# Three arms by row count in a mixture-of-experts loop, each stage in two branches, weight splits seven halves ahead

## Chip, cores, metric

One core of one Trainium2 chip. The metric is the device time of one execution in microseconds; lower is better. The time before is the median of three runs.

## What is computed

A block with a gated-MLP and a linear-attention half, then a routed mixture of 64 experts with D = 1024 and an inner width of 512, over 2048 tokens, two experts for each token, everything in float32. The part that matters:

```python
def hier_moe(t, wrg, brg, wre, bre, w1, w3, w2):
    ...
    gate = p_top * jax.nn.softmax(l_top, axis=-1)
    expert = g_idx * EXPERTS_PER_GROUP + e_local
    ...
    def expert_block(args):
        xblk, e = args
        hblk = jax.nn.silu(xblk @ w1[e]) * (xblk @ w3[e])
        return hblk @ w2[e]
    ...
    yb = yb * buf_gate[:, None].astype(yb.dtype)
    return jax.ops.segment_sum(yb, buf_tok, num_segments=T + 1)[:T]
...
h = h + g2 * y.reshape(Bn, S, D)
return rmsnorm(h, g_final)
```

## The kernel before

Up to about 1040 us the kernel computes the two mixing halves and the routing: for each expert a list of its token rows (`idx`), its gates, and the number of blocks of 128 rows (`nblk`). The loop over 64 experts follows, and from about 2363 us the final norm. The change lies in the loop.

**An expert's matrices.** `w_e` holds 12 k-tiles of 128 x 1024 for each expert: eight for up (w1 and w3 side by side, 512 columns each) and four for down. SP loads each k-tile into one of 28 raw tiles in rotation (`wload`, L611). Half a tile, 512 columns, is one *half*: 16 halves in up, 8 in down.

**Splits.** Float32 products are made of three matmuls in a rounded format, fp32r. ScalarE rounds a raw half to `wh` (L80), VectorE subtracts to get the rest `wl` (L81); both lie in a ring of eight pairs. The rows are split likewise: `xhe` and `xle` for up, `hhe` and `hle` for down. `mm3` (L84 to L86) then issues xh wh, xh wl and xl wh into one PSUM bank. `need(p)` issues all splits up to half p; `block` calls it four halves ahead of the matmuls.

**Order.** One pass is up(e+1), weight loads, the count of the next expert, a gather of rows by POOL (`gath`, L1162), down(e). `xprep` (L1195 to L1199) transposes the gathered rows of expert e+2 on TensorE and splits them; it stands in the middle of down(e), ahead of its fifth half. `htr` (L1203) transposes the gated result of expert e+1 ahead of the seventh half, and `hsplit` (L1207, L1208) splits it in the middle of the next up. `glu` (L1211, L1212) is silu on ScalarE and a product on VectorE; `yevac` (L1217) scales down's result by the gate; `scat` (L1220) adds its rows into DRAM, an indirect DMA issued by POOL. Each engine runs its instructions in this order.

**Arms.** `up` and `down` have two versions behind a branch on `nblk[e]` that every engine takes: `one` for at most 128 rows, `two` for a second block, whose matmuls follow three halves behind and use the same splits. `PA`, `PY`, `TP` and `TH` are pairs of PSUM banks.

Of the kernel before, what the change touches and what calls it, by code (L numbers as in the profile page):

```python
# [8 lines left out]
F32 = mybir.dt.float32  # L9
# [8 lines left out]
P = 128  # L18
# [12 lines left out]
def kernel(ctx: ExitStack, tc: tile.TileContext, a: dict, out: bass.AP):  # L31
# [1147 lines left out]
    vec.tensor_scalar(nblk, ci_, 7, None, op0=OP.logical_shift_right)  # L1179
    most = wk.tile([1, 1], I32, name="most")  # L1180
# [45 lines left out]
    LA = R - LAG - 1  # L1226
# [5 lines left out]
    def need(p):  # L1232
        nonlocal nsp
        while nsp <= min(p, len(hseq) - 1):
            e, k, i = hseq[nsp]
            split_w(W[e, k][:, i * 512:(i + 1) * 512], *ring[nsp % R])
            nsp += 1

    def both(two, one):

        nonlocal nsp
        n0 = nsp
        two()
        n1, nsp = nsp, n0
        yield
        one()
        assert nsp == n1
# [8 lines left out]
    def block(base, n, outs, hls, at):  # L1256

        for q in range(n + (LAG if len(outs) > 1 else 0)):
            if q < n:
                need(base + q + LA)  # L1260
                if q in at:
                    at[q]()
# [27 lines left out]
    def rest():  # L1290
# [22 lines left out]
    def up(e):  # L1313

        at = {4: lambda: hsplit(TH[0], hx)} if e else {}
        base = hpos[e, 0, 0]

        def two():
            xprep(xq[e % 2], rows2(e), PY)
            block(base, 2 * KD, (PA, TP), (xhl, rows2(e)), at)  # L1320
            glu(PA, sh)
            glu(TP, sh2[e % 2])

        def one():
            block(base, 2 * KD, (PA,), (xhl,), at)
            glu(PA, sh)

        g = both(two, one)
        with tc.If(NB_[e] > 1, preferred_fallthrough_block=False) as f:
            next(g)  # L1330
        with f.Else():
            next(g, None)

    def down(e):

        base = hpos[e, KD, 0]
        at = {}
        if e + 2 < NE:
            at[4] = lambda: xprep(xg[(e + 2) % 3], xhl, TP)
# [3 lines left out]
        def two():
            htr(sh2[e % 2], TH[1])
            hsplit(TH[1], hx2)
            block(base, 2 * KF, (PY, PA), (hx, hx2), at)
            yevac(PA, col(gate, NE + e), y2)
            scat(y2, col(idx, NE + e))

        def one():  # L1350
            block(base, 2 * KF, (PY,), (hx,), at)

        g = both(two, one)
        with tc.If(NB_[e] > 1, preferred_fallthrough_block=False) as f:
            next(g)
        with f.Else():
            next(g, None)
# [6 lines left out]
    need(LA - 1)  # L1364
# [48 lines left out]
def _layout(inp):  # L1413
# [29 lines left out]
    z["w_e"] = np.concatenate([w13, w2], axis=1).transpose(0, 2, 1, 3).reshape(NE, P, 12 * D)  # L1443
# [30 lines left out]
```

## Time and profile before

| what | us |
|---|---|
| median of 3 runs | 2416.13 (2415.8 to 2416.62) |
| the profiled execution | 2418.95 |
| its span | 2417.3 |
| PE busy | 2279.6 (94%) |
| DVE busy | 1929.6 (80%) |
| ACT busy | 1438.4 (60%) |
| POOL busy | 727.9 (30%) |
| mean granted TensorE clock | 0.969 |

Engines are PE (TensorE), DVE (VectorE), ACT (ScalarE), POOL (GpSimd) and SP (which issues DMAs). A pipelined instruction shows longer than the distance to the next one's start; that distance is what it costs its engine. A row's bracket holds the idle time just before it and what ended it. [...] Busy shares over the span mix the phases; the loop is read from its own windows.

### The profile page before, as it was taken

How to read it: one execution, taken by the hardware profiler on the slowest of the kernel's cores; microseconds unless marked ns; L12 is line 12 of the kernel's file. 1: busy time of each engine (PE TensorE's matmuls, PEld its weight loads, DVE VectorE, ACT ScalarE, POOL GpSimd, SP SyncE). 2: the span in 40 equal slices, each digit the busy share in tenths (PEclk: the TensorE clock that was granted, in tenths of full speed). 3: DMA queues.
4: the chain of work that ended last, by engine and by line, in shares of the span. 5: the costliest groups of instructions: out<-in, count | busy, mean ns of one | idle time of the engine just before them, and what ended most of it. 6: DMA issues, size and time to landing. Idle time of an engine off the chain costs nothing.

```text
span 2417.3 us, 40083 instructions
## 1 busy us (share of the span) xinstructions
PE 2279.6 (94%) x11932; PEld 1879.8 (78%) x11932; DVE 1929.6 (80%) x4302; ACT 1438.4 (60%) x2731; POOL 727.9 (30%) x602
## 2 busy tenths in 40 slices
PE   8999999999999899889999999999999999999980
PEld 3888888978777788778777888888777788888870
DVE  4555566567786788789887899999686699999986
ACT  3544443433323222378776788888575588888873
POOL 1123311147673122237521122323131232322220
PEclk9899999999999999989999999999999999999995
DMA  7333332256664654589998899999996799999947
GB/s 273 110 102 100 106 108 97 97 179 213 221 221 155 233 209 177 184 309 377 332 305 263 285 379 371 367 353 347 328 322 192 219 360 371 369 357 357 364 144 295
DMA packets 193220, 613.42 MB, mean 254 GB/s; under 512 B 36557, under 2 KB 36685, under 8 KB 192854
## 3 DMA queue, kind: packets, MB, share of 16 engines
q1 hardware_dynamic: 152358, 516.56, 58.8%
q0 software_dynamic: 38048, 87.95, 12.3%
q10 hardware_dynamic: 2448, 4.46, 0.5%
q8 instruction: 178, 2.92, 0.5%
q14 instruction: 188, 1.54, 0.2%
HBM read 547.42 MB, written 102.28 MB: 269 GB/s over the span
## 4 chain that ended last, share of the span: by engine, by line
PE 33%; DVE 12%; DMA 7%; issue 5%; ACT 0%; DVEq 0%; another core or an unknown queue 0%; SPq 0%; POOLq 0%; ACTq 0%; POOL 0%
DVE wl L81 9%; PE pa L84 6%; PE pa L86 6%; PE pa L85 6%; DMA we<-in_w_e_dram 4%; PE py L86 3%; PE py L84 3%; PE py L85 3%; DMA accD<-y,idx 2%; PE tpe L1195 1%; DVE y L1217 1%; PE tpe L85 1%; PE tpe L84 1%; PE tpe L86 1%; DMA hf<-accD 1%
## 5 line engine op out<-in xcount | busy, mean ns | idle before, releaser
L81 DVE TENSOR_TENSOR wl<-we,wh 128x512 fp32r<-128x512 f32 x1536 | 954.2, 682 | 83.6 <-ACT wh L80 77.0
L80 ACT ACTIVATE wh<-we 128x512 fp32r<-128x512 f32 x1536 | 892.4, 630 | 146.9 <-DVE wl L81 46.4
L84 PE MATMUL pa<-wh,xhe 128*128 128x512 f32 x1024 | 403.4, 394 | 9.5 <-ACT wh L80 6.3
L86 PE MATMUL pa<-wh,xle 128*128 128x512 f32 x1024 | 399.9, 391 | 0.0
L85 PE MATMUL pa<-wl,xhe 128*128 128x512 f32 x1024 | 399.5, 390 | 0.0
L1220 POOL DMA_INDIRECT accD<-y,idx x71 | 238.8, 3364 | 530.7 <-DVE y L1217 446.7
L84 PEld LDWEIGHTS pa<-wh,xhe 128*128 128x128 f32 x1024 | 192.3, 188 | 69.9 <-issue 28.5
L86 PEld LDWEIGHTS pa<-wh,xle 128*128 128x128 f32 x1024 | 192.3, 188 | 40.7
L85 PEld LDWEIGHTS pa<-wl,xhe 128*128 128x128 f32 x1024 | 192.5, 188 | 37.6
L84 PE MATMUL py<-wh,hhe 128*128 128x512 f32 x512 | 213.7, 417 | 6.9 <-ACT wh L80 6.4
L1162 POOL DMA_INDIRECT xg<-hnD,idx x64 | 93.5, 1461 | 417.2 <-DVE wl L81 143.2
L86 PE MATMUL py<-wh,hle 128*128 128x512 f32 x512 | 202.9, 396 | 1.6 <-issue 1.3
L85 PE MATMUL py<-wl,hhe 128*128 128x512 f32 x512 | 201.3, 393 | 3.2 <-DVE wl L81 3.2
L86 PEld LDWEIGHTS py<-wh,hle 128*128 128x128 f32 x512 | 97.3, 190 | 25.7 <-issue 3.4
L349 POOL TENSOR_SCALAR sc<-sc,dec 64x128 f32<-64x128 f32 x140 | 111.4, 795 | 19.1 <-PE po L682 7.8
L84 PEld LDWEIGHTS py<-wh,hhe 128*128 128x128 f32 x512 | 97.5, 190 | 24.8 <-issue 6.3
L85 PEld LDWEIGHTS py<-wl,hhe 128*128 128x128 f32 x512 | 97.8, 191 | 16.0 <-issue 0.2
L1070 POOL DMA_INDIRECT tabD<-pair,ri x32 | 70.0, 2187 | 91.3 <-DMA tabD<-pair,ri 58.8
L86 PE MATMUL pmx<-hi,mld 128*128 128x512 f32 x224 | 89.6, 400 | 5.6 <-DVE mld L81 5.6
L1217 DVE SCALAR_TENSOR_TENSOR y<-py,gate,g2b 128x512 f32<-128x512 f32 x128 | 89.7, 740 | 4.1 <-PE py L86 4.1
L84 PE MATMUL pmx<-hi,mhd 128*128 128x512 f32 x224 | 91.4, 408 | 0.4 <-ACT mhd L80 0.4
L85 PE MATMUL pmx<-lo,mhd 128*128 128x512 f32 x224 | 88.6, 396 | 0.0
(417 smaller groups left out, 4660.1 us busy)
## 6 DMA issues: line engine op xcount, KB each, us to landing
we<-in_w_e_dram SPq DMA_DIRECT2D x765, 512.0 KB
wt<-in_w_modB_dram SPq DMA_DIRECT2D x32, 512.0 KB
kve<-kveD SPq DMA_DIRECT2D x48, 256.0 KB
wt<-in_w_modA_dram SPq DMA_DIRECT2D x16, 512.0 KB
x<-in_x_dram SPq DMA_DIRECT2D x16, 512.0 KB
xD<-xf POOLq DMA_DIRECT2D x32, 256.0 KB
mfd<-mxD SPq DMA_DIRECT2D x16, 512.0 KB
xd<-in_x_dram SPq DMA_DIRECT2D x16, 512.0 KB
```

Of the source, the lines that this page charges most:

```text
L80: act.activation(hi, raw, AF.Copy)
L81: vec.tensor_tensor(lo, raw, hi.bitcast(F32), op=OP.subtract)
L84: pe.matmul(o, lh, wh, start=start, stop=False)
L85: pe.matmul(o, lh, wl, start=False, stop=False)
L86: pe.matmul(o, ll, wh, start=False, stop=stop)
L349: pool.tensor_scalar(s1[64:128, hs], s0[64:128, hs], dec[64:128, ci, h:h + 1], None, op0=OP.mult)
L1070: pool.indirect_dma_start(out=tabD, out_offset=bass.IndirectOffsetOnAxis(ap=ri[:, i:i + 1], axis=0), in_=pair[:, i], in_offset=None)
L1162: pool.indirect_dma_start(out=x, out_offset=None, in_=hnD, in_offset=bass.IndirectOffsetOnAxis(ap=ix, axis=0), bounds_check=S - 1, oob_is_ ...
L1195: pe.transpose(four(tp[c // 4])[:, c % 4], x[:, c * P:(c + 1) * P], ident)
L1217: vec.scalar_tensor_tensor(y[:, c], py[i], gt, g2b[:, c], op0=OP.mult, op1=OP.mult)
L1220: pool.indirect_dma_start(out=accD, out_offset=bass.IndirectOffsetOnAxis(ap=ix, axis=0), in_=y, in_offset=None, bounds_check=S - 1, oob_is ...
```

## The change

A third arm, `few`, serves experts with at most 64 rows. `xx` holds the low part of the first 64 rows beside the high part of all 128, so that one matmul with `wh` or `wl` (`block2`) makes both products: two matmuls a half instead of three. The result's two halves of partitions are added in `glu2`. The low part comes into `xx` by a POOL copy at the end of `xprep`, for every expert. In down, the last halves are neither split nor rounded: plain float32 matmuls out of the raw tiles with `hf`, a float32 copy of the transposed gated rows; four of eight halves in few, two in one, none in two. Each stage is cut in two branches of half the length. Splits go up to seven halves ahead (four in two); one or two halves of up are held back until after the silu (`held`). `w_e` is laid out with each k-tile in one piece, and 27 raw tiles rotate instead of 28. `nhalf` counts blocks of 64 rows. In the changed kernel the lines are: branches L1263 and L1264, `few`'s matmuls L1306, `glu2`'s three VectorE operations L1312, L1314 and L1316, `xprep`'s L1206, its POOL copy L1208, `hsplit` L1219, `glu` L1224, `yevac` L1229, `scat` L1232, the counts L1320 and L1328.

```diff
-    NW, NR = 25, 28
+    NW, NR = 25, 27
...
-            eng.dma_start(out=W[e, k], in_=a["w_e"][e, :, k * D:(k + 1) * D])
+            eng.dma_start(out=W[e, k], in_=a["w_e"][e, k])
...
-    xhl = [wk.tile([P, KD, P], F32R, name=n) for n in ("xhe", "xle")]
+    LO, HI = slice(0, P // 2), slice(P // 2, P)
+    xx = wk.tile([P, KD, P // 2 + P], F32R, name="xhe")
+    xhl = [xx[:, :, P // 2:], wk.tile([P, KD, P], F32R, name="xle")]
...
+        if hl is xhl:
+            pool.tensor_copy(xx[:, :, LO], xl[:, :, LO].bitcast(F32))
...
         act.activation(hh, four(th), AF.Copy)
+        if th is TH[0]:
+            act.activation(hf, four(th)[:, 2:4], AF.Copy)
...
-    LA = R - LAG - 1
...
-    def both(two, one):
+    def arms(e, two, one, few):
...
+        with tc.If(NB_[e] > 1, preferred_fallthrough_block=False) as f:
+            with tc.If(NB_[e] > 2, preferred_fallthrough_block=False) as g:
+                arm(two)
+            with g.Else():
+                arm(one)
+        with f.Else():
+            arm(few)
...
+    def block(base, n, span, top, outs, hls, at=(), raw=0):
...
+            need(base + min(q + R - 1 - lag, top), raws)
...
+                if p < n - raw:
+                    mms(o[p % 2], hl, p // 2, p % 2, n // 2, ring[(base + p) % R])
+                else:
+                    e, k, i = hseq[base + p]
+                    pe.matmul(o[i], hf[:, p // 2 - 2], W[e, k][:, i * 512:(i + 1) * 512], start=False,
+                              stop=p // 2 == n // 2 - 1)
...
+    def block2(base, n, span, top, at):
+
+        for q in range(*span):
+            need(base + min(q + R - 1, top))
+            if q in at:
+                at[q]()
+            for j, w in enumerate(ring[(base + q) % R]):
+                pe.matmul(PA[q % 2], xx[:, q // 2, 0:P], w, start=q < 2 and j == 0, stop=q // 2 == n // 2 - 1 and j == 1)
+
+    def glu2(t, between):
+
+        act.activation(t[HI], PA[0][HI], AF.Copy)
+        act.activation(sh[HI], PA[1][HI], AF.Copy)
+        vec.tensor_tensor(sh[LO], PA[0][LO], t[HI], op=OP.add)
+        act.activation(sh[LO], sh[LO], AF.Silu)
+        vec.tensor_tensor(t[LO], PA[1][LO], sh[HI], op=OP.add)
+        between()
+        vec.tensor_tensor(sh[LO], sh[LO], t[LO], op=OP.mult)
...
     def up(e):
...
+        ends = {KD: KD + R - 2, n: n + 3}
+        for span in ((0, KD), (KD, n)):
+            top = ends[span[1]]
+            held = lambda: need(base + n + 3)
...
+            def few():
+                block2(base, n, span, top - (span[1] == n), at)
+                if span[1] == n:
+                    glu2(sh2[e % 2], held)
+
+            arms(e, two, one, few)
...
     def down(e):
...
+        for span in ((0, KF), (KF, n)):
+            top = span[1] + R - 2
...
+            arms(e, two, lambda: block(base, n, span, top, (PY,), (hx,), raw=2),
+                 lambda: block(base, n, span, top, (PY,), (hx,), raw=4))
+            if span[0] == 0 and e + 2 < NE:
+                xprep(xg[(e + 2) % 3], xhl, TP)
         if e + 1 < NE:
-            at[6] = lambda: htr(sh, TH[0])
...
+            htr(sh, TH[0])
...
-    need(LA - 1)
+    need(R - 2)
```

Three places show the order of the instructions. First VectorE at the end of up, before (`wl` are splits, `she` is the gated product):

```order
L81 TENSOR_TENSOR wl_11208<-we_9492,wh_11207 128x512
L81 TENSOR_TENSOR wl_11210<-we_9492,wh_11209 128x512
L81 TENSOR_TENSOR wl_11212<-we_9494,wh_11211 128x512
L81 TENSOR_TENSOR wl_11214<-we_9494,wh_11213 128x512
L1212 TENSOR_TENSOR she<-she,pa_11183 128x512
L1329 UNCONDITIONAL_BRANCH
```

and now, in the few arm of the second branch of up:

```order
L1263 COMPARE_AND_BRANCH
L81 TENSOR_TENSOR wl_11225<-we_11146,wh_11224 128x512
L81 TENSOR_TENSOR wl_11211<-we_11175,wh_11210 128x512
L81 TENSOR_TENSOR wl_11213<-we_11175,wh_11212 128x512
L81 TENSOR_TENSOR wl_11215<-we_11177,wh_11214 128x512
L1312 TENSOR_TENSOR she<-pa_11180,sh_11206 64x512
L1314 TENSOR_TENSOR sh_11206<-pa_11181,she 64x512
L81 TENSOR_TENSOR wl_11217<-we_11177,wh_11216 128x512
L1316 TENSOR_TENSOR she<-she,sh_11206 64x512
L1263 UNCONDITIONAL_BRANCH
```

Two additions of half height have come in ahead of the product, and one split, the held one, stands between them and it.

Second VectorE in down around `xprep` (`xle`), before:

```order
L81 TENSOR_TENSOR wl_11222<-we_11179,wh_11221 128x512
L81 TENSOR_TENSOR wl_11208<-we_8756,wh_11207 128x512
L1199 TENSOR_TENSOR xle<-tpe_11184,xhe 128x512
L1199 TENSOR_TENSOR xle<-tpe_11185,xhe 128x512
L81 TENSOR_TENSOR wl_11210<-we_8756,wh_11209 128x512
L81 TENSOR_TENSOR wl_11212<-we_8758,wh_11211 128x512
L81 TENSOR_TENSOR wl_11214<-we_8758,wh_11213 128x512
L1354 UNCONDITIONAL_BRANCH
```

and now, with the few arm's second branch of down behind it:

```order
L1206 TENSOR_TENSOR xle<-tpe_11182,xhe 128x512
L1206 TENSOR_TENSOR xle<-tpe_11183,xhe 128x512
L1263 COMPARE_AND_BRANCH
L81 TENSOR_TENSOR wl_11217<-we_8948,wh_11216 128x512
L81 TENSOR_TENSOR wl_11219<-we_9128,wh_11218 128x512
L81 TENSOR_TENSOR wl_11221<-we_9128,wh_11220 128x512
L81 TENSOR_TENSOR wl_11223<-we_9130,wh_11222 128x512
L1263 UNCONDITIONAL_BRANCH
```

`xprep` has moved out of the branch to the seam between its two; four splits follow the last `xle` instead of three, and the two `y` come next in both kernels.

Third POOL in down, before (`xq` and the first `accD` are for a second block, in branches of their own):

```order
L1162 DMA xq_10938<-hnD,idx 128x1024
L1272 UNCONDITIONAL_BRANCH
L1354 COMPARE_AND_BRANCH
L1354 ISA
L1354 UNCONDITIONAL_BRANCH
L1220 DMA accD<-y_10939,idx 2048x1024
L1354 UNCONDITIONAL_BRANCH
L1220 DMA accD<-y_11206,idx 2048x1024
```

and now:

```order
L1162 DMA xq_11164<-hnD,idx 128x1024
L1322 UNCONDITIONAL_BRANCH
L1263 COMPARE_AND_BRANCH
L1263 UNCONDITIONAL_BRANCH
L1264 COMPARE_AND_BRANCH
L1264 UNCONDITIONAL_BRANCH x2
L1208 CAST xhe<-xle 128x8x64
L1263 COMPARE_AND_BRANCH
L1263 ISA
L1263 UNCONDITIONAL_BRANCH
```

The copy stands behind the gather and between the two branches of down, ahead of the scatter.

## Rows read from the trace of the kernel before

**Rows 1.** This is the table of windows of the expert loop and of the end: window, its length, busy us (x instructions) of PE, PEld, DVE, ACT and POOL, then PEclk (granted clock of TensorE), DMA share, GB/s.

```profile
1400.00:1500.00 100.00, 98.90 (x462) 80.45 (x461) 100.00 (x166) 88.21 (x158) 30.45 (x11) 1.00 1.01 376
2375.00:2412.00 37.00, 0.00 (x0) 0.00 (x0) 33.53 (x111) 16.11 (x29) 0.00 (x0) 0.50 0.98 396
```

**Rows 2.** This is the timeline of VectorE over one expert with at most 128 rows: start us, us from the first start to the last end, engine, line, operation, out<-in, count.

```profile
1405.11 3.09 DVE L81 TENSOR_TENSOR wl<-we,wh 128x512 fp32r<-128x512 f32 x5
1408.12 0.68 DVE L1208 TENSOR_TENSOR hle<-th,hhe 128x512 fp32r<-128x512 f32 x1
1408.72 6.70 DVE L81 TENSOR_TENSOR wl<-we,wh 128x512 fp32r<-128x512 f32 x11
1415.35 0.68 DVE L1212 TENSOR_TENSOR she<-she,pa 128x512 f32<-128x512 f32 x1
1415.94 3.09 DVE L81 TENSOR_TENSOR wl<-we,wh 128x512 fp32r<-128x512 f32 x5
1418.96 1.28 DVE L1199 TENSOR_TENSOR xle<-tpe,xhe 128x512 fp32r<-128x512 f32 x2
1420.15 1.89 DVE L81 TENSOR_TENSOR wl<-we,wh 128x512 fp32r<-128x512 f32 x3
1421.96 1.40 DVE L1217 SCALAR_TENSOR_TENSOR y<-py,gate,g2b 128x512 f32<-128x512 f32 x2
1423.28 1.88 DVE L81 TENSOR_TENSOR wl<-we,wh 128x512 fp32r<-128x512 f32 x3
```

**Rows 3.** This is the timeline of TensorE for the same expert: three matmuls of up, the eight transposes of `xprep`, the four of `htr`, and the seam from down to up.

```profile
1413.75 0.39 PE L84 MATMUL pa<-wh,xhe 128*128 128x512 f32 x1
1413.98 0.39 PE L85 MATMUL pa<-wl,xhe 128*128 128x512 f32 x1
1417.15 1.03 PE L1195 MATMUL tpe<-cst,xg 128*128 128x128 f32 x8
1417.94 0.47 PE L84 MATMUL py<-wh,hhe 128*128 128x512 f32 x1
1419.41 0.60 PE L1203 MATMUL th<-cst,she 128*128 128x128 f32 x4
1419.77 0.47 PE L84 MATMUL py<-wh,hhe 128*128 128x512 f32 x1
1421.00 0.40 PE L86 MATMUL py<-wh,hle 128*128 128x512 f32 x1
1421.59 0.47 PE L84 MATMUL pa<-wh,xhe 128*128 128x512 f32 x1 [0.19 <-ACT wh L80]
```

**Rows 4.** This holds two groups of POOL's instructions by line (count | busy us, mean ns | idle before and its releasers), ScalarE's splits in 1400 to 1500 us in the same form, and two scatters from POOL's timeline.

```profile
L149 POOL CAST trs<-cst 128x512 fp32r<-128x512 f32 x1 | 0.8, 764 | 31.1 <-DMA cst<-in_cst_dram 31.1
L1121 POOL COPY ht<-sh2T 128x1024 f32<-128x1024 f32 x1 | 1.2, 1222 | 0.0
...
L80 ACT ACTIVATE wh<-we 128x512 fp32r<-128x512 f32 x135 | 78.0, 630 | 3.5 <-DVE wl L81 1.1
...
1405.47 4.19 POOL L1220 DMA_INDIRECT accD<-y,idx  x1 [7.29 <-DVE y L1217]
...
1312.32 1.59 POOL L1220 DMA_INDIRECT accD<-y,idx  x1 [12.19 <-DVE y L1217]
```

**Rows 5.** This is the timeline of TensorE in short stretches of 602.9 to 603.4 and 603.4 to 603.8 us: plain f32 matmuls, two at a time.

```profile
602.46 1.13 PE L739 MATMUL pm<-macc,cst 128*128 128x512 f32 x2
...
602.99 1.02 PE L739 MATMUL pm<-macc,cst 128*128 128x512 f32 x2
```

**Rows 6.** This is the timeline of POOL and of VectorE at 570 to 573 us.

```profile
570.27 1.29 POOL L350 TENSOR_TENSOR sc<-sc,kbb 64x512 f32<-64x512 f32 x1 [0.92 <-DMA kbb<-kvbD]
...
570.68 2.04 DVE L81 TENSOR_TENSOR xl<-xfc,xh 128x512 fp32r<-128x512 f32 x2
```

**Rows 7.** This is the timeline of ScalarE in the same expert as rows 2.

```profile
1417.79 1.09 ACT L1198 ACTIVATE xhe<-tpe 128x512 fp32r<-128x512 f32 x2 [0.39 <-PE tpe L1195]
```

**Rows 8.** This is the timeline of TensorE at its stands; in brackets the idle time before the row and what ended it.

```profile
58.43 0.30 PE L213 MATMUL tp<-cst,x 128*128 128x128 f32 x1 [2.60 <-DVE x L195]
...
204.08 0.42 PE L254 MATMUL pz<-cst,kz 128*96 128x128 f32 x1 [2.19 <-DVE kz L245]
...
259.87 0.28 PE L254 MATMUL pz<-cst,kz 128*96 128x128 f32 x1 [1.73 <-DVE kz L245]
...
531.86 0.77 PE L680 MATMUL po<-kve,at 128*128 128x128 f32 x2 [1.79 <-issue]
...
1741.03 0.59 PE L85 MATMUL py<-wl,hhe 128*128 128x512 f32 x1 [3.21 <-DVE wl L81]
1741.41 0.63 PE L86 MATMUL py<-wh,hle 128*128 128x512 f32 x1
1741.84 0.63 PE L84 MATMUL py<-wh,hhe 128*128 128x512 f32 x1
```

**Rows 9.** This is the table of windows at the end of or right behind the first four of these stands, in the columns of rows 1.

```profile
58.40:61.80 3.40, 3.10 (x18) 2.68 (x19) 2.64 (x5) 2.16 (x5) 0.00 (x0) 1.00 0.00 0
259.90:263.30 3.40, 3.40 (x23) 3.14 (x24) 1.73 (x7) 0.00 (x0) 0.56 (x1) 1.00 0.34 130
531.90:535.30 3.40, 3.40 (x16) 2.07 (x16) 0.76 (x2) 0.00 (x0) 1.53 (x3) 0.50 1.05 311
203.80:207.20 3.40, 3.12 (x11) 2.86 (x12) 2.03 (x9) 0.00 (x0) 0.56 (x1) 0.50 0.05 18
```

More of the change, by code (lines that the diff above doesn't have):

```diff
@@ L1230, with need @@
     nsp = 0
-    def need(p):
+    def need(p, raw=()):
         nonlocal nsp
@@ L1235, in need, with arm @@
             e, k, i = hseq[nsp]
-            split_w(W[e, k][:, i * 512:(i + 1) * 512], *ring[nsp % R])
+            if nsp not in raw:
+                split_w(W[e, k][:, i * 512:(i + 1) * 512], *ring[nsp % R])
             nsp += 1
-    def both(two, one):
+    def arms(e, two, one, few):
         nonlocal nsp
[L1242 to L1247, printed above, removed]
+        n0, done = nsp, []
+        def arm(f):
+            nonlocal nsp
+            nsp = n0
+            f()
+            done.append(nsp)
+        with tc.If(NB_[e] > 1, preferred_fallthrough_block=False) as f:
[5 more added lines that the diff above has]
+            arm(few)
+        assert len(set(done)) == 1
     def mms(o, hl, k, i, nk, ring_):
@@ L1254, in rows2 @@
         return [t.rearrange("p (k n) -> p k n", k=KD) for t in (xgr[e % 3], xqr[e % 2])]
[L1256 to L1262, printed above, removed]
+    def block(base, n, span, top, outs, hls, at=(), raw=0):
+        raws = range(base + n - raw, base + n)
+        lag = LAG if len(outs) > 1 else 0
+        for q in range(span[0], span[1] + lag):
+            need(base + min(q + R - 1 - lag, top), raws)
+            if q in at:
+                at[q]()
@@ L1285, in again @@
             for i in range(2):
-                pool.dma_start(out=raw, in_=a["w_e"][e, :, k * D + i * 512:k * D + (i + 1) * 512])
+                pool.dma_start(out=raw, in_=a["w_e"][e, k, :, i * 512:(i + 1) * 512])
                 split_w(raw, wh, wl)
@@ L1315, in up @@
         at = {4: lambda: hsplit(TH[0], hx)} if e else {}
[L1316 to L1332, printed above, removed]
@@ L1334, in down @@
-    def down(e):
[L1336 to L1339, printed above, removed]
-        if e + 1 < NE:
-            at[6] = lambda: htr(sh, TH[0])
[L1343 to L1357, printed above, removed]
+        base, n = hpos[e, 0, 0], 2 * KD
@@ new lines, in up, with two, one @@
+        ends = {KD: KD + R - 2, n: n + 3}
+        for span in ((0, KD), (KD, n)):
+            top = ends[span[1]]
+            held = lambda: need(base + n + 3)
+            def two():
+                if span[0] == 0:
+                    xprep(xq[e % 2], rows2(e), PY)
+                block(base, n, span, top, (PA, TP), (xhl, rows2(e)), at)
+                if span[1] == n:
+                    glu(PA, sh)
+                    glu(TP, sh2[e % 2])
+            def one():
+                block(base, n, span, top - (span[1] == n), (PA,), (xhl,), at)
+                if span[1] == n:
+                    glu(PA, sh, held)
+            def few():
+                block2(base, n, span, top - (span[1] == n), at)
+                if span[1] == n:
+                    glu2(sh2[e % 2], held)
+            arms(e, two, one, few)
@@ new lines, in down, with two @@
+    def down(e):
+        base, n = hpos[e, KD, 0], 2 * KF
+        for span in ((0, KF), (KF, n)):
+            top = span[1] + R - 2
+            def two():
+                if span[0] == 0:
+                    htr(sh2[e % 2], TH[1])
+                    hsplit(TH[1], hx2)
+                block(base, n, span, top, (PY, PA), (hx, hx2))
+                if span[1] == n:
+                    yevac(PA, col(gate, NE + e), y2)
+                    scat(y2, col(idx, NE + e))
+            arms(e, two, lambda: block(base, n, span, top, (PY,), (hx,), raw=2),
+                 lambda: block(base, n, span, top, (PY,), (hx,), raw=4))
+            if span[0] == 0 and e + 2 < NE:
+                xprep(xg[(e + 2) % 3], xhl, TP)
+        if e + 1 < NE:
+            htr(sh, TH[0])
```

27 lines of the change are left out of this document (18 added, 9 removed).

## Prediction, made before the changed kernel ran

> **What bounds the kernel now.** I read the windows of the expert loop first, then one expert on VectorE, ScalarE and TensorE. In 1400 to 1500 us VectorE is busy 100.00 of 100 us and TensorE 98.90 at full clock, while ScalarE has 12 us to spare and POOL 70 [rows 1]. So two engines bound it together. One expert with at most 128 rows takes VectorE from 1405.11 to 1423.28, 18.17 us, without a gap: 24 `wl`, 2 `xle`, 1 `hle`, 1 product, 2 `y`, that is 30 operations [rows 2]. Eleven `wl` followed by the product start 6.63 us after the first (1408.72 to 1415.35), so one costs 0.602 us of VectorE's time though it shows 0.68; a `y` costs 0.66 to 0.70. Check: 28 x 0.602 + 2 x 0.66 = 18.18. TensorE in the same time: 72 matmuls that start 0.227 apart (16.3), eight transposes 0.79, four transposes 0.36, and the seam between down and up, 0.59 instead of 0.23 [rows 3]: about 18. Both must get shorter for a gain. The weight stream is a third floor close by: 376 GB/s over 1400 to 1500, while the end of the program reaches 396 [rows 1]; 376 x 18.17 is 6.83 MB an expert, so about 17.25 us at 396.
>
> How many experts take which arm follows from the reference's routing on its own inputs: 41 experts have at most 64 rows (few), 16 have 65 to 128 (one), 7 more (two).
>
> **Few, what goes.** Four splits of 24 go and two operations of the gating are added: 28 for 30 on VectorE, -2 x 0.602 = **-1.20 us** an expert, to 16.97. TensorE loses 16 matmuls in up (-3.6) and 12 in down, replaced by four plain f32 ones at 0.43 (602.99 to 603.42, [rows 5]): 18 - 3.6 - 2.7 + 1.8 = about 13.5 us, no longer a bound by its sum. ScalarE gains two half-height copies and the 128x256 copy `hf` for four splits of 0.63 less: covered by its 12 us of room in 100 [rows 1], and without that it would still come out shorter.
>
> **Few, the gating.** The new order is add, add, held split, product. The chain is add 0.68, silu 0.60, the held half's `wh` 0.63 and then its `wl`: 1.91 us after the first add starts, of which the second add covers 0.60 and the first one's own slot 0.60. So VectorE stands about **+0.72**. Bounds: 0 if the silu is issued early enough, 0.9 with hand-over delays of 0.1 each.
>
> **Few, the copy on POOL.** This is the term I hold decisive. Each `xprep` now ends with a POOL copy of 128 x 8 x 64 out of `xle`, and the next few arm's first matmul waits for it. The nearest row is a 128x512 cast on POOL, 0.76 us; the largest copy there, 128x1024, took 1.22 [rows 4]. But when does it get its turn? The scatter on POOL that starts at 1405.47 takes 4.19 us, the one at 1312.32 only 1.59 [rows 4]. Under the slow one VectorE runs five `wl` in a row, until 1408.12 [rows 2]. 1408.12 + 1.59 is 1409.71, and the slow scatter ends at 1409.66: POOL stood until the unbroken run of two-SBUF-operand subtractions was over, and VectorE lost nothing. In the change, four `wl` follow the last `xle` directly, and only then the two `y`, which read PSUM. So the copy starts about when `y` does.
>
> Times from the end of the eight transposes, t (1417.94 in rows 3). ScalarE's second `xhe` ended 0.94 later (1417.79 + 1.09, [rows 7]); `xle` starts at t+1.0, the four `wl` run to t+4.0, the copy to t+4.8. TensorE meanwhile needs 1.8 for four plain halves and 0.36 for `htr`: done at t+2.2. So it now stands about 2.3 us between down and up (2.6, less what the two new seams take). Its first half ends at t+5.25, the ninth split can only then refill that slot (`wh` 0.63, then `wl`) at t+6.25, and VectorE, through with `y` and one `wl` at t+5.9, stands **+0.4**. So far the few arm is 16.97 + 0.72 + 0.4 = 18.09 instead of 18.17: -0.08 x 41 = **-3.3 us**. With a copy of 1.22 it is +0.4 each (+16), with half the gating's stall -0.4 (-16).
>
> [...]
>
> **Few, the clock.** TensorE has stood for 1.79 and 2.19 us, and right after each the granted clock was 0.50 (1.2 GHz); after 1.73 it stayed 1.00 (2.4 GHz), and once after 2.60 too [rows 8, 9]. After 3.21 its matmuls start 0.43 apart, which is 1.2 GHz [rows 8]. A stand of 2.3 in every few arm lies on the falling side of most of these: I take 7 in 10 of 41, 29 times. Behind the stand of 2.19 it was low for the 3.4 us from 203.80 to 207.20 [rows 9]; that I take. At 0.43 a matmul, a half of the few arm is 0.85, longer than VectorE's 0.602, and 3.4 us cost TensorE 1.7 us. It had little slack: up needs 16 x 0.454 plus a seam, from t+4.8 to t+12.4, and the gating's first add could run at t+13.5, after TensorE's end, ScalarE's copies (0.60) and hand-overs. So about **+1.3** each time; bounds 0.6 (the slack larger) and 2.6 (two such stretches). 29 x 1.3 = **+37.7 us**.
>
> **One.** 28 operations too (22 splits), floor 16.97; but TensorE binds it: six matmuls at 0.227 go, two plain halves at 0.43 and about 0.1 for changing over come, -0.40, and two more seams cost 0 to 0.36 each. I take -0.2 x 16 = **-3.2** (bounds -6 and +5).
>
> **Two.** Nothing is saved, two more seams at 0.36 each: 0.7 x 7 = **+5** (0 to +15: the stand of 3.21 in such an arm, [rows 8], may move or recur, since all engines carry more branches).
>
> **Other edits.** The new weight layout, 27 raw tiles for 28 and more branches on SP: nothing, as ScalarE's splits stood 3.5 us in 100 and never for a weight DMA [rows 4]; without that cover the stream's 17.25 us is the limit, which is below 18.09. Three more splits before the loop, the counts: **+1** (0 to 2).
>
> **The sum.** 2418.95 (profiled execution) - 3.3 + 37.7 - 3.2 + 5 + 1 = 2456.2. The profiled execution is 2.8 above the median, so the forecast is **2453 us**, slower; its own range 2430 to 2490.
>
> **Rivals.**
> 1. *The clock holds.* Same waits, no 37.7: 2416. For it: the stand of 2.60 without a fall, and that seams may break the stand up. With the bounds of copy and gating, 2400 to 2434.
> 2. *The copy finds its turn at once* (VectorE has a gap there, as ScalarE's `wh` may be late): then few is 16.97 + 0.72 + 0.1 for seams = 17.8, -0.37 x 41 = -15, and with the other terms 2404, faster. Against it: VectorE shows no gap around `xle` now.
> 3. *The copy in time, and splits 7 ahead also hide the gating and the seams*: few falls to the stream's 17.25, one by 0.4: 2418.95 - 37.7 - 6.4 + 1 - 2.8 = 2373, faster. For it: TensorE gets 4 us of slack, and splits further ahead need it less.
> [...]
> 5. *The change does little of what it says*: the few arm saves what it adds, 2416.
>
> [...]
>
> **Chances.** Forecast 0.41; rival 1 0.18 (0.07 faster, 0.07 same, 0.04 slower); rival 2 0.15; rival 3 0.13; rival 4 0.08; rival 5 0.05. Within 0.2% (2411.3 to 2420.9; about what a measurement of this kernel can tell from no change) 0.12, faster 0.35, slower 0.53. The signs are split, so the range has to reach both: 2370 leaves out the lower half of rival 3, 2495 the case of two low stretches each time.
>
> **What would show it.** Right: in few arms TensorE stands about 2 us on POOL's copy before the first up matmul, the copy starts with `y`, the granted clock there is 0.50 for part of up, VectorE is no longer at 100%. Wrong: the copy ends before `y` starts (rivals 2, 3), `wl` after `xle` at 1.3 instead of 0.68 (rival 4), or a clock of 1.00 behind such stands (rival 1).

## Result, and the profile after

The changed kernel takes 2440.44 us (median of 4, 2434.81 to 2441.97) against 2415.97 beside it. The ratio estimated from the runs is 1.0087 of the time before, 95% interval 1.0074 to 1.010; the two medians alone would give 1.0101. It is slower, inside the range and 13 us under the forecast. Its profiled execution took 2439.76 us, 20.8 more than the one before. The sign and the size came out; the largest term did not, and others stood in for it, which is luck.

The table of windows, in the columns of [rows 1]:

```profile
1400.00:1500.00 100.00, 88.53 (x359) 60.49 (x357) 95.06 (x155) 79.62 (x151) 40.49 (x18) 0.98 1.00 368
1500.00:1600.00 100.00, 88.77 (x360) 61.08 (x360) 96.52 (x158) 79.67 (x153) 45.72 (x18) 1.00 0.98 357
```

Neither engine is full any more: TensorE stands 11 us in 100, VectorE 3.5 to 5, and the clock, 0.98 and 1.00, hardly fell. So most of the loop is held by a chain between the engines, not by one engine's sum. VectorE over one few expert between two others (timeline; answers to [rows 2]):

```profile
1466.18 3.08 DVE L81 TENSOR_TENSOR wl<-we,wh 128x512 fp32r<-128x512 f32 x5
1469.19 0.68 DVE L1219 TENSOR_TENSOR hle<-th,hhe 128x512 fp32r<-128x512 f32 x1
1469.79 4.29 DVE L81 TENSOR_TENSOR wl<-we,wh 128x512 fp32r<-128x512 f32 x7
1474.11 0.68 DVE L1312 TENSOR_TENSOR she<-pa,sh 64x512 f32<-64x512 f32 x1
1474.71 0.67 DVE L1314 TENSOR_TENSOR sh<-pa,she 64x512 f32<-64x512 f32 x1
1476.01 0.69 DVE L81 TENSOR_TENSOR wl<-we,wh 128x512 fp32r<-128x512 f32 x1 [0.62 <-ACT wh L80]
1476.62 0.68 DVE L1316 TENSOR_TENSOR she<-she,sh 64x512 f32<-64x512 f32 x1
1477.22 1.88 DVE L81 TENSOR_TENSOR wl<-we,wh 128x512 fp32r<-128x512 f32 x3
1479.03 1.27 DVE L1206 TENSOR_TENSOR xle<-tpe,xhe 128x512 fp32r<-128x512 f32 x2
1480.22 2.48 DVE L81 TENSOR_TENSOR wl<-we,wh 128x512 fp32r<-128x512 f32 x4
1482.63 1.40 DVE L1229 SCALAR_TENSOR_TENSOR y<-py,gate,g2b 128x512 f32<-128x512 f32 x2
1483.95 0.68 DVE L81 TENSOR_TENSOR wl<-we,wh 128x512 fp32r<-128x512 f32 x1
```

From 1466.18 to 1483.95 it is 17.77 us: 28 operations, and one stand of 0.62 at the held split. POOL's copy in the same expert and the first copy of the loop (timeline):

```profile
1480.43 2.74 POOL L1208 CAST xhe<-xle 128x512 fp32r<-128x512 f32 x1 [5.42 <-DVE xle L1206]
...
1049.10 0.61 POOL L1208 CAST xhe<-xle 128x512 fp32r<-128x512 f32 x1 [3.59 <-DMA hnD<-xd]
```

and all of them (groups by line; count | busy us, mean ns):

```profile
L1208 POOL CAST xhe<-xle 128x512 fp32r<-128x512 f32 x64 | 131.5, 2054 | 324.2 <-DVE xle L1206 320.7 <-DMA hnD<-xd 3.6
```

Alone the copy takes 0.61. Behind `xle` it takes 2.74, to 1483.17. Its own 0.61 would then begin at 1482.56, about when the slot of the fourth `wl` (from 1482.03) ends: it stood through the run of four, as the forecast had it. Forty of the 64 copies take so long. Twenty-four end sooner, 22 of them in 0.93 to 0.98, and in 16 of the 24 one split beside the copy takes 1.02 instead of 0.60. One of these, with VectorE's splits beside it (timeline):

```profile
1660.67 2.90 DVE L81 TENSOR_TENSOR wl<-we,wh 128x512 fp32r<-128x512 f32 x4
...
1660.90 0.93 POOL L1208 CAST xhe<-xle 128x512 fp32r<-128x512 f32 x1 [3.19 <-DVE xle L1206]
```

The four splits take 2.90 instead of 2.48, as one of them lasts longer beside the copy: this is the sign that the forecast's last line gives to rival 4. It happens in all seven places where up of a one expert runs beside down of a few one. What lets the copy in is not shown: in most of these places VectorE had stood 0.29 ahead of `xle`, but a copy got in also where it had not stood at all (1699.46).

TensorE at the seam behind the first of these copies, and the same place of a one expert behind a one (timeline; answers to [rows 3]):

```profile
1478.21 3.60 PE L1296 MATMUL py<-we,hfe 128*128 128x512 f32 x8
1481.64 0.60 PE L1212 MATMUL th<-cst,she 128*128 128x128 f32 x4
1483.28 0.47 PE L1306 MATMUL pa<-wh,xhe 128*128 128x512 f32 x1 [1.03 <-POOL xhe L1208]
...
1698.20 1.88 PE L1296 MATMUL py<-we,hfe 128*128 128x512 f32 x4
1699.91 0.60 PE L1212 MATMUL th<-cst,she 128*128 128x128 f32 x4
1701.91 0.47 PE L84 MATMUL pa<-wh,xhe 128*128 128x512 f32 x1 [1.39 <-DVE wl L81]
```

Two things to see. Four plain halves show eight matmuls and last 3.43 us (1478.21 to 1481.64), two show four: **the program's one plain f32 matmul stands in the trace as two**, 0.86 us a half. And a one expert, which does not wait for the copy, stands too, for a split: 1.39 here, where the copy made one split 0.42 longer, and 0.82 one expert earlier (1682.24).

**Where the 20.9 us up to the last `y` lie.** Between the last `y` of expert e-1 and that of e, TensorE runs up(e+1) and down(e). I sorted these distances by the two arms (from VectorE's timeline of `y`):

| down(e), up(e+1) | pairs | before, median us | after, median us | sum of differences |
|---|---|---|---|---|
| few, few | 30 | 18.17 | 17.77 | -9.5 |
| few, one | 7 | 18.16 | 18.69 | +3.7 |
| one, few | 6 | 18.16 | 18.98 | +4.9 |
| one, one | 7 | 18.16 | 19.18 | +7.7 |
| two, few | 3 | 30.32 | 23.97 | -13.1 |
| others with a two | 9 | | | +14.6 |
| last expert | 1 | 6.73 | 7.91 | +1.2 |
| all up to the last `y` of the first expert | | 1074.4 | 1085.9 | +11.5 |

Of the last line 3.0 us are there before the loop (the router's matmul at 1020.15 before, 1023.11 after), in code that the change does not touch; the other 8.5 are the loop's start.

### The profile page after: what moved, and what is told of

It reads as the page before. It is cut to its first block, busy times and chain, and to the rows that moved or that the text cites. A ratio compares the mean times of both kernels' runs of the same rounds, so it can differ in the third digit from the quotient of the medians.

```text
span 2437.7 us, 40053 instructions
## 1 busy us (share of the span) xinstructions
PE 2210.8 (91%) x11080; PEld 1719.3 (71%) x11080; DVE 1875.2 (77%) x4193; ACT 1366.3 (56%) x2684; POOL 788.1 (32%) x665
## 3 DMA queue, kind: packets, MB, share of 16 engines
q14 instruction: 257, 2.11, 0.2%
## 4 chain that ended last, share of the span: by engine, by line
PE 34%; DVE 7%; DMA 7%; issue 4%; ACT 3%; POOL 3%; ACTq 1%; DVEq 0%; another core or an unknown queue 0%; SPq 0%; POOLq 0%
PE pa L1306 8%; DVE wl L81 4%; PE pa L84 4%; PE pa L86 4%; PE pa L85 4%; DMA we<-in_w_e_dram 4%; POOL xhe L1208 3%; ACT wh L80 3%; PE py L85 2%; PE py L1296 2%; PE py L86 2%; PE tpe L1202 2%; PE py L84 1%; PE tpe L85 1%; PE tpe L84 1%
## 5 line engine op out<-in xcount | busy, mean ns | idle before, releaser
L81 DVE TENSOR_TENSOR wl<-we,wh 128x512 fp32r<-128x512 f32 x1343 | 850.6, 687 | 157.5 <-ACT wh L80 155.3
L80 ACT ACTIVATE wh<-we 128x512 fp32r<-128x512 f32 x1343 | 762.9, 628 | 231.5 <-PE pa L1306 55.7
L1306 PE MATMUL pa<-wh,xhe 128*128 128x512 f32 x656 | 265.0, 404 | 48.2 <-POOL xhe L1208 40.6
L1232 POOL DMA_INDIRECT accD<-y,idx x71 | 204.4, 2879 | 217.4 <-DVE y L1229 128.2
L1306 PE MATMUL pa<-wl,xhe 128*128 128x512 f32 x656 | 265.6, 405 | 0.0
L1208 POOL CAST xhe<-xle 128x512 fp32r<-128x512 f32 x64 | 131.5, 2054 | 324.2 <-DVE xle L1206 320.7
L1306 PEld LDWEIGHTS pa<-wh,xhe 128*128 128x128 f32 x656 | 126.0, 192 | 83.1 <-issue 57.1
L1296 PE MATMUL py<-we,hfe 128*128 128x512 f32 x392 | 177.8, 593 | 0.0
L84 PE MATMUL py<-wh,hhe 128*128 128x512 f32 x316 | 131.1, 415 | 25.6 <-ACT she L1311 10.7
L1306 PEld LDWEIGHTS pa<-wl,xhe 128*128 128x128 f32 x656 | 126.0, 192 | 39.6 <-DVE wl L81 13.1
L86 PE MATMUL pa<-wh,xle 128*128 128x512 f32 x368 | 146.0, 397 | 0.0
L85 PE MATMUL py<-wl,hhe 128*128 128x512 f32 x316 | 132.1, 418 | 14.7 <-DVE wl L81 14.0
L86 PE MATMUL py<-wh,hle 128*128 128x512 f32 x316 | 125.2, 396 | 0.2 <-DVEq L1263 0.2
L1296 PEld LDWEIGHTS py<-we,hfe 128*128 128x128 f32 x392 | 71.6, 191 | 68.2 <-issue 64.7
L1229 DVE SCALAR_TENSOR_TENSOR y<-py,gate,g2b 128x512 f32<-128x512 f32 x128 | 89.5, 738 | 5.3 <-PE py L1296 5.2
## 6 DMA issues: line engine op xcount, KB each, us to landing
we<-in_w_e_dram SPq DMA_DIRECT2D x766, 512.0 KB, 11.9
```

The costliest lines, as they stand in the source:

```text
L80: act.activation(hi, raw, AF.Copy)
L81: vec.tensor_tensor(lo, raw, hi.bitcast(F32), op=OP.subtract)
L84: pe.matmul(o, lh, wh, start=start, stop=False)
L85: pe.matmul(o, lh, wl, start=False, stop=False)
L86: pe.matmul(o, ll, wh, start=False, stop=stop)
L1208: pool.tensor_copy(xx[:, :, LO], xl[:, :, LO].bitcast(F32))
```

## Experiments

All ratios are to the kernel before; pairs are medians as in the table, in us. The last column runs from the first transposes of `xprep` to the last `y` of the first expert. What lies ahead of these transposes is the same code in all kernels, and still they start between 1039.3 us (e1) and 1052.1 us (e3). So a few us between two times, or between two first `y`, can come from there; pairs and the last column are free of it.

| kernel | time | ratio, interval | few, few | one, one | one, few | start |
|---|---|---|---|---|---|---|
| before | | 1 | 18.17 | 18.16 | 18.16 | 34.1 |
| changed | 2440.44 | 1.0087 (1.0074 to 1.010) | 17.77 | 19.18 | 18.98 | 42.6 |
| e1 | 2432.24 | 1.0062 (1.004 to 1.0085) | 17.78 | 19.15 | 19.02 | 41.5 |
| e2 | 2466.78 | 1.0205 (1.0176 to 1.0234) | 17.78 | 20.38 | 20.21 | 44.1 |
| e3 | 2523.6 | 1.0432 (1.0399 to 1.0465) | 18.80 | 19.54 | 22.82 | 42.9 |
| e4 | 2448.65 | 1.0136 (1.0107 to 1.0165) | 18.74 | 18.13 | 19.52 | 40.9 |
| e5 | 2463.81 | 1.0209 (1.0181 to 1.0238) | 18.47 | 18.28 | 19.68 | 44.2 |
| e6 | 2449.51 | 1.0143 (1.0125 to 1.0161) | 18.27 | 18.43 | 19.47 | 42.3 |
| e8 | 2417.18 | 1.0001 (0.9991 to 1.0011) | 18.17 | 18.17 | 18.17 | 35.3 |
| e9 | 2423.43 | 1.0033 (1.0017 to 1.005) | 17.77 | 18.11 | 18.98 | 40.5 |
| e10 | 2445.04 | 1.0114 (1.0094 to 1.0134) | 18.15 | | | |
| e11 | 2402.04 | 0.9938 (0.9921 to 0.9956) | 18.07 | 18.07 | 18.07 | 35.2 |
| e12 | 2393.28 | 0.9889 (0.9871 to 0.9906) | 17.89 | 17.88 | 17.89 | 34.0 |

**e1, the copy on ScalarE.**

```diff
-        if hl is xhl:
-            pool.tensor_copy(xx[:, :, LO], xl[:, :, LO].bitcast(F32))
+    def lowcopy():
+        act.activation(xx[:, :, LO], xhl[1][:, :, LO].bitcast(F32), AF.Copy)
...
+            at = {6: lowcopy} if span[0] and e + 2 < NE else {}
```

> The low part is copied into xx by ScalarE, after the third split of the second branch of down, instead of by POOL; nothing else changes. In the changed kernel two few experts in a row are 17.77 us apart, POOL's copy takes 2.74 us there and TensorE stands 1.03 us for it. Theory (the copy waits for the run of subtractions, but the few arm is held by VectorE, whose idle time is 0.62 at the gating and about 0.1 elsewhere): TensorE's stand goes below 0.4, the distance falls by at most 0.1 to 0.2, -4 to -8 us over 41 experts, and 4 to 5 us more at the start, where TensorE stood 4.52 for the copy behind POOL's other work: 2425 to 2433. Rival (the copy sets the few arm's period through TensorE): the distance falls by about 1.0, to the weight stream's floor of 17.25 or below: 2395 to 2415.

TensorE no longer stands for the copy (timeline):

```profile
2031.86 0.60 PE L1213 MATMUL th<-cst,she 128*128 128x128 f32 x4
2032.47 0.47 PE L1307 MATMUL pa<-wh,xhe 128*128 128x512 f32 x1
```

and two few experts are 17.78 apart as with the copy on POOL. In the steady few arm the theory holds: the copy's long wait is off the path, and VectorE's 16.97 with its stand at the gating sets 17.77. At the start it does not. TensorE still stands there, now with no releaser named:

```profile
1044.42 0.77 PE L1307 MATMUL pa<-wh,xhe 128*128 128x512 f32 x1 [3.18 <-issue]
```

From the first transposes to the first expert's `y` only 1.1 us went, not 4 to 5. Of the 8.8 us between the two profiled executions 4.0 lie ahead of the transposes, in code that is the same. The rest is mainly two things. The few, one pairs fell from 18.69 to 18.30, as the copy no longer gets in between the splits. And the three few pairs that took 18.5 to 18.8 behind a one expert now take 17.78.

**e2, no plain halves in one.**

```diff
-            arms(e, two, lambda: block(base, n, span, top, (PY,), (hx,), raw=2),
+            arms(e, two, lambda: block(base, n, span, top, (PY,), (hx,), raw=0),
```

> The one arm splits all eight halves of down and has no plain f32 halves; few keeps its four. Theory (a plain f32 matmul is carried out as two, so that a plain half costs TensorE 0.86 us and not 0.43, against 0.68 for three fp32r matmuls, and the one arm is bound by TensorE): 0.36 to 0.5 us less for each of 16 one experts, the distance of two one experts in a row 19.1 to 19.5 now, 18.7 to 19.1 then: -5 to -9 us in all. Rival (the one arm is held by its seams and the held split's chain on ScalarE and VectorE, 2.08 us of VectorE's idle time there): two more splits on VectorE, +0.0 to +1.2 each: 0 to +15 us.

The theory fell: 1.20 more between two ones, just two `wl`, and 26 us in all, beyond the rival's 15. TensorE waits for VectorE there:

```profile
1719.57 0.47 PE L84 MATMUL pa<-wh,xhe 128*128 128x512 f32 x1 [2.42 <-DVE wl L81]
```

The stand ahead of up between two ones, 0.82 and 1.39 in the changed kernel, is 2.36 and 2.42 here. So the one arm is not bound by TensorE's sum but by a wait for a split at the seam, and every `wl` on the way to it counts.

**e3, up in one branch.**

```diff
-        for span in ((0, KD), (KD, n)):
+        for span in ((0, n),):
```

> Up is one branch of 16 halves again, down stays in two. Theory (a branch costs TensorE a seam of about 0.36 us where TensorE binds, and short branches are what removed the stands of 3.2 and 4.6 us of two-block experts): one experts 0.2 to 0.4 shorter, few experts the same within 0.05, two-block experts 0 to 7 us longer in some places: -6 to +10 in all. Rival (the seams cost nothing, since each engine runs ahead of the branch): one experts unchanged within 0.05.

Far worse than either theory: few pairs went from 17.77 to anything between 17.77 and 24.8. TensorE behind such a branch:

```profile
1444.39 0.77 PE L84 MATMUL py<-wh,hhe 128*128 128x512 f32 x1 [6.47 <-issue]
1444.95 0.63 PE L85 MATMUL py<-wl,hhe 128*128 128x512 f32 x1
1445.38 0.63 PE L86 MATMUL py<-wh,hle 128*128 128x512 f32 x1
```

A stand of 6.47 that nothing on the other engines ended (the 3.21 in [rows 8] was ended by a split), and then about half the pace (matmuls 0.43 apart; 0.23 at 1395 in the same run). Eight stands of this kind, 5.5 to 6.5 long, lie in the loop; the changed kernel's longest is 2.6. Here three arms are only affordable in short branches (2523.6 against 2440.44). What TensorE waited for at these stands, no row names.

**e4, no splits in the second branch of down.**

```diff
-            top = span[1] + R - 2
+            top = KF + R - 2
```

> The second branch of down issues no splits; the four splits that stood between the last xle and y come in the next up, so splits are three ahead of TensorE at the start of up instead of seven. Theory (POOL's copy takes 2.05 us on average, 2.74 in few experts, because it waits for the unbroken run of four subtractions, and only 0.61 by itself): its mean falls below 1.0 us, and TensorE no longer stands for it, but for the first splits of up instead. The time: between -5 and +25, as what the copy gives back is lost where the splits are late. Rival (the copy is slow by itself, its input being strided): its mean stays above 1.8 us.

```profile
L1208 POOL CAST xhe<-xle 128x512 fp32r<-128x512 f32 x64 | 39.4, 615 | 340.2 <-DVEq L1263 196.7 <-DVEq L1264 82.2 <-DVE xle L1206 57.6
```

The copies now take 0.61 on average, the longest 0.93: the run of subtractions was the whole difference. And the one pairs, of which nothing was expected, fell from 19.18 to 18.13, while few pairs rose to 18.74. That pointed to what the seam waits for.

**e5, the four splits behind the branch.**

```diff
-            top = span[1] + R - 2
+            top = KF + R - 2
...
+        need(base + n + R - 2)
         if e + 1 < NE:
             htr(sh, TH[0])
```

> The four splits of the second branch of down are issued behind that branch instead of inside it; the order of each engine's work is the same, and splits are still seven ahead. Theory (the first matmul of up waits, through the counts that the branch leaves behind, for the last but one split inside the branch before it, which in the changed kernel is a split for half 5 of up and comes 1.4 us after TensorE is ready): two one experts in a row go from 19.1 to 19.7 us down to 18.0 to 18.5, two few experts stay at 17.77 within 0.1, as there POOL's copy ends at the same time and VectorE binds: 14 to 25 us less in all, 2415 to 2427. Rival (the one arm is longer by TensorE's own work and seams): less than 0.2 each, 2436 to 2442.

Half right. One pairs fell to 18.28 as the theory has it (the seven lie between 17.75 and 19.31), with the splits still seven ahead: what matters is that none stands in the branch. But few pairs rose by 0.70 and the total by 23. VectorE behind the last `xle`, and POOL (timeline):

```profile
2053.59 2.69 DVE L81 TENSOR_TENSOR wl<-we,wh 128x512 fp32r<-128x512 f32 x4 [0.41 <-DVEq L1263]
...
2053.32 0.61 POOL L1208 CAST xhe<-xle 128x512 fp32r<-128x512 f32 x1 [5.42 <-DVEq L1263]
```

At the empty branch VectorE stands 0.41 on its own sequencer; in that hole POOL's copy starts at once, and then VectorE loses another 0.21 (2.69 for four `wl` instead of 2.48). That is the longer split beside the copy again, at half of the 0.42 above.

**e6, e5 with the copy on ScalarE.**

```diff
-        need(base + n + R - 2)
+        need(base + n + R - 3)
+        if e + 2 < NE:
+            lowcopy()
+        need(base + n + R - 2)
```

> As the kernel with the four splits behind the branch, and the low part is copied into xx by ScalarE after the third of these splits instead of by POOL. Theory (both are small waits of different arms and add up; the copy cost 5 us in the first expert and a few tenths where a few expert stands beside a one): 5 to 10 us below the kernel with the splits behind the branch alone, two few experts in a row 17.6 to 17.8. Rival (without the wait for the copy the few arm runs at VectorE's 16.97 or the weight stream's 17.25): two few experts 17.0 to 17.4 apart, 15 to 30 us below it.

Few pairs 18.27, which neither forecast had: the 0.2 beside the copy went, the stand at the empty branch stayed. 14 us below e5, more than the theory's 10.

**e7, six plain halves in few.**

```diff
-                 lambda: block(base, n, span, top, (PY,), (hx,), raw=4))
+                 lambda: block(base, n, span, top, (PY,), (hx,), raw=6))
```

> As the kernel with both (splits behind the branch, copy on ScalarE), and few keeps six of down's eight halves plain instead of four. Two more splits of VectorE's 0.602 us go in each few expert; TensorE gets 2 x (0.86 - 0.68) more. Theory (VectorE binds the few arm): two few experts in a row at 17.77 less 1.2, unless the weight stream's floor comes first, so 17.0 to 17.4, 15 to 30 us less over 41 experts. Rival (the few arm is bound by the gating's chain through TensorE and ScalarE, not by VectorE's sum): less than 0.3 each, 0 to 12 us.

2864.76 us, which answers nothing: a raw tile goes back to the loads when its split is due, here ahead of the plain matmuls that read it.

**e8, the layout of the weights alone, in the kernel before.**

```diff
-    NW, NR = 25, 28
+    NW, NR = 25, 27
...
-            eng.dma_start(out=W[e, k], in_=a["w_e"][e, :, k * D:(k + 1) * D])
+            eng.dma_start(out=W[e, k], in_=a["w_e"][e, k])
```

> The kernel before with one part of the change alone: w_e with each k-tile in one piece, and 27 raw tiles in rotation instead of 28. Theory (the splits never waited for the weight stream): no difference, ratio 0.998 to 1.002. Rival (the stream is near its limit and one raw tile less or other addresses cost): 2 to 10 us longer, with idle time of ScalarE's splits put down to a weight DMA.

No difference. In the kernel before, this part of the change costs and gives nothing.

**e9, two splits in the branch and two behind it.** e6 with:

```diff
-            top = KF + R - 2
+            top = KF + R - 2 + (2 if span[0] else 0)
...
-    need(R - 2)
+    need(3)
     xprep(xg[0], xhl, TP)
```

> The changed kernel with the copy on ScalarE, two of the four splits inside the second branch of down and two behind it, and four splits instead of seven ahead of the first expert's transposes. Theory (an empty branch makes VectorE stand 0.41 to 0.48 us, which cost the few arm with all four splits behind the branch 0.5; four splits inside make up wait; with two inside neither happens): two few experts in a row 17.77 to 17.9, two one experts 18.1 to 18.6, the first expert 2 to 4 us earlier than with the copy on ScalarE alone: 2412 to 2424. Rival (any branch without enough work for the time that the jump takes leaves VectorE idle, or the wait is for the branch's end whatever it holds): few at 18.1 or more, or one at 19 or more: 2430 to 2450.

`need(3)` is the four splits ahead of the first transposes. Both parts held: few 17.77, one 18.11. Of the seven one pairs four lie at 17.9 to 18.1; the three right behind a few, one pair still take 19.0 to 19.1. The start gained 1.0 over e1, not 2 to 4. At 2423.43 most of the loss is gone, and it is still 0.33% above the kernel before: the start takes 6.4 more, and a one beside a few still costs 18.98.

**e10, six plain halves again.** e9 with e7's edit, and raw tiles given back one later. The split of halves at the end of up follows expert e+1's arm, though they belong to e's down; where the two differ, two halves of down are left out. Only few pairs are read.

> As the kernel with two splits inside and two behind, and few keeps six of down's eight halves plain; the raw tiles are given back one later. In the run of this idea before, the second k-tile of down was loaded anew ahead of its plain matmuls, so that they read another tile, and its time said nothing. Theory (VectorE binds the few arm): two few experts in a row 17.77 less 1.2 for two splits, plus at most 0.3 for the gating, so 16.6 to 17.3 with the weight stream's floor at 17.25: 15 to 35 us below the kernel with four. Rival (TensorE, with 0.86 us a plain half, or the gating's chain binds by then): less than 0.3 each, 0 to 12 us.

Worse than the rival, which had a small gain: 18.15 instead of 17.77, and 19.3 to 20.2 in ten of the 30. TensorE and VectorE in one of them:

```profile
2090.47 1.88 PE L1297 MATMUL py<-we,hfe 128*128 128x512 f32 x4
2092.19 1.04 PE L1202 MATMUL tpe<-cst,xg 128*128 128x128 f32 x8
...
2093.46 1.29 DVE L1206 TENSOR_TENSOR xle<-tpe,xhe 128x512 fp32r<-128x512 f32 x2 [0.78 <-ACT xhe L1205]
```

Two plain halves, 1.72 us, now stand ahead of the transposes, and VectorE waits for what follows them.

**e11, two plain halves in the kernel before**, with 27 raw tiles to make room (e8 shows that these cost nothing).

```diff
-                if 0 <= p < n:
+                if 0 <= p < n - raw:
                     mms(o[p % 2], hl, p // 2, p % 2, n // 2, ring[(base + p) % R])
+                elif n - raw <= p < n:
+                    e, k, i = hseq[base + p]
+                    pe.matmul(o[i], hf[:, 0], W[e, k][:, i * 512:(i + 1) * 512], start=False, stop=True)
...
-            block(base, 2 * KF, (PY,), (hx,), at)
+            block(base, 2 * KF, (PY,), (hx,), at, 2)
```

> The kernel before with one part of the change alone: the last two halves of down plain f32 in the arm for up to 128 rows (57 experts), with 27 raw tiles for the room. Theory (a plain f32 matmul runs as two passes, so a plain half takes TensorE 0.86 us against 0.68; before, TensorE and VectorE bind together): the distance of two experts goes from 18.16 to 18.4 to 18.7, +14 to +30 us. Rival (the prediction's price, 0.43 a plain half): TensorE 0.40 less and VectorE 1.20 less, 17.7 to 17.9, -15 to -25 us.

Between the two: 18.07. The windows:

```profile
1400.00:1500.00 100.00, 100.00 (x457) 79.28 (x456) 94.14 (x155) 82.27 (x152) 23.41 (x13) 1.00 1.01 372
```

and VectorE's timeline:

```profile
1421.93 1.29 DVE L1200 TENSOR_TENSOR xle<-tpe,xhe 128x512 fp32r<-128x512 f32 x2 [1.01 <-ACT xhe L1199]
```

TensorE is full and VectorE stands 1.0 an expert: of VectorE's 1.20 only 0.10 came through. At 0.43 a half TensorE would have had room, so the price of 0.86 is right, and TensorE before took 18.07 - 0.36 = 17.7, where my sum had about 18. The 50 pairs without a two give 8.2 us of the 15.8 of this run. More, 11.5, comes from the two, few pairs, 24.7 instead of 30.3: the stands of [rows 8] are gone there too, and no run shows why. The time up to the first expert's last `y` takes 4.0 back.

**e12, one plain half in the kernel before.** e11 with 1 for 2.

> The kernel before with only the last half of down plain f32 in the arm for up to 128 rows, and 27 raw tiles. With two plain halves the distance of two experts was 18.07, TensorE busy all the time and VectorE standing 0.99 an expert. Theory (TensorE binds there, and a plain half takes it 0.18 us more than a split one): 17.85 to 17.95 with one plain half, VectorE's sum being 17.57; 57 x 0.15 to 0.2, so 6 to 12 us below the kernel with two, 2390 to 2397. Rival (the distance is set by the order in which VectorE and TensorE wait for each other, and what VectorE gives is lost whatever TensorE needs): 18.07 to 18.16, no gain or up to 6 us longer.

```profile
1400.00:1500.00 100.00, 100.00 (x463) 81.11 (x462) 98.91 (x164) 86.24 (x160) 23.15 (x12) 1.00 1.01 368
```

18.07 less 0.18 is 17.89: exactly 0.86 - 0.68 for the half given back. TensorE is full, VectorE at 98.91. This version is faster than both kernels, at 0.9889 (0.9871 to 0.9906), with one part of the change and no third arm. Of its gain the 50 pairs give 16.0 us; 11.9 are again the two, few pairs.

## Why the prediction was right, and where it was not

The time came out by luck, the mechanism only in part. By the forecast's own signs the copy's turn and VectorE's room came as told. But TensorE stood 1.03 and not about 2 us in a few pair, and the clock behind that stand stayed at 1.00, which was the sign of rival 1.

- **Few, what goes**: right, 28 operations at 0.602.
- **The gating**: +0.72 forecast, 0.62 measured. The hand-over, 0.1 in the upper bound, is 0.03 from the first add's end to the silu (1474.79 to 1474.82).
- **The copy's turn**: right for the few pairs. It stood through the run of four `wl` in 29 of 30 (2.74 against 0.61; e4: 0.61 on average). It cost nothing in a steady few pair (e1), where I had +0.4; so a few pair gives 0.40 and not 0.08. In 16 other places the copy got in, and a split took 1.02 instead of 0.60; two subtractions beside a POOL operation in [rows 6] (2.04; 1.29 for the next two) and the four in e5 (2.69 instead of 2.48) show the like. The other 40 copies stood through the splits, and the splits kept their 0.60. What decides between the two, no run shows.
- **The step that failed is the price of a plain half**, "four plain f32 ones at 0.43". Each is two in the trace; two records of [rows 5] belong to one matmul of the program, and I took each record for one. Four plain halves take 3.43, not 1.8; so TensorE is busy while the copy waits, and stands 1.03 instead of 2.3 in a few pair.
- **The clock**, my +37.7, therefore fell in the loop only where the stand was long, 2.04 and more (behind 2.11 at 1722.31 and 2.73 at 1197.75 it held too), as behind a one expert (timeline of TensorE):

```profile
1428.93 0.77 PE L1306 MATMUL pa<-wh,xhe 128*128 128x512 f32 x1 [2.58 <-POOL xhe L1208]
1429.49 0.63 PE L1306 MATMUL pa<-wl,xhe 128*128 128x512 f32 x1
1429.92 0.63 PE L1306 MATMUL pa<-wh,xhe 128*128 128x512 f32 x1
```

  The fall is there (2.58, then matmuls 0.43 apart, the granted clock 0.51 from 1428.60 to 1432.00), in a few places instead of 29: behind three of four such stands the next few pair took 18.5 to 18.8. In e1, where these stands are 0.6 to 1.6, it took 17.78. The forecast's 1.2 GHz is an estimate: 512 columns every 0.43 us behind the 3.21 of [rows 8], with 0.50 granted from 1741.00 to 1744.40, are about 1.2 a ns, taken as one a cycle; 2.4 is its double. No term uses them.
- **One**: -3.2 forecast; the three lines with a one give +16.3, by three causes. *One, few* (+4.9) is VectorE's sum, which I had taken by experts and not by pairs: down of a one splits two halves more than down of a few, and up of a few has the two additions, so that VectorE runs 30 operations as before and stands 0.62 besides. 17.77 and two splits of 0.60 make 18.97; measured 18.98, in e9 too. *Few, one* (+3.7) is mainly the copy that gets in between the splits; with it on ScalarE 1.0 is left (e1). *One, one* (+7.7) is a wait. The first matmul of up waits for the last but one split inside the branch of down before it (e2, e4, e5, e9). Running seven ahead, that split is one that up needs only much later. Why that one: in the two arm the branch ends with two `y` that empty the bank which up writes, and it seems that the other arms pass on the same two counts with their last operations. The trace shows for what TensorE waits; this reason is argued.
- **Two**: +5 forecast, +1.5 measured, as two large parts: -13.1 where the stands of [rows 8] are gone, +14.6 elsewhere, which no run took apart.
- **The start**: +1 forecast, +8.5 measured. I had costed nothing there but three splits and the counts. The first copy sits on POOL's queue behind the loop's other preparations:

```profile
1049.81 0.76 PE L1306 MATMUL pa<-wh,xhe 128*128 128x512 f32 x1 [4.52 <-POOL xhe L1208]
```

  But with the copy on ScalarE TensorE still stands 3.18 (e1), and only 1.1 of the 8.5 goes; with four splits ahead instead of seven another 1.0 goes (e9). The other 6.4 are open.

Against the sum of 2456.2 the profiled execution came out 16.4 lower: clock -37.7 and few -6.2 (-9.5, with its falls of the clock, for -3.3), one +19.5, start +7.5, two -3.5, and 4.2 from the stretch ahead of the loop and the last expert; that is 16.2, the rest is rounding and the end. The range held because terms that I put too low replaced the one that I put too high.

## What to carry to other kernels

Count a new operation by a row whose program text you have counted too: one matmul of the program need not be one in the trace. Where experts of different arms overlap, count by pairs. Before work is moved ahead of a branch, ask what the first instruction behind the branch waits for; if it waits for the branch's end, everything that was moved in has to be done first. When two engines bind a loop together, as before this change, a small share moved between them can give more than a new arm: one half of eight gave 16.0 us in 50 pairs (e12), the few arm 9.5 in 30.

## What the runs showed of the hardware that was not expected

- A plain f32 matmul of 128x512 showed as two records and took 0.86 us at a granted clock of 1.00 (1478.20 to 1481.70); three fp32r ones took 0.68 (0.227 apart).
- POOL stood through a whole run of subtractions with two SBUF operands in 40 of 64 cases: 2.74 us for a copy of 0.61 behind four, while those kept their 0.60. In 16 others it got in between them, and one subtraction took 1.02. With a hole of 0.41 ahead of the run, POOL was first, took its 0.61, and the run of four took 2.69 instead of 2.48.
- A branch without work on VectorE cost it 0.41 us (e5); with two or four splits in it VectorE did not stand there (e9, the changed kernel).
- With three arms of 16 halves TensorE stood 5.5 to 6.5 us eight times in the loop with no releaser (e3), matmuls 0.43 apart behind the 6.47; with arms of 8 halves the longest such stand was 2.6 (1888.87).
